# Hybrid encoder trunk: pre-norm token factors applied behind the input and up projections instead of ahead of them

## The chip, the cores and the metric

The kernel runs on one core of one Trainium2 chip. The core has a matrix engine (PE, with its weight loads shown as PEld), a vector engine (DVE), a scalar engine (ACT), a general engine (POOL) and an engine that here only issues transfers (SP). Each works through its own instructions in order and waits on semaphores for the others. Products land in PSUM banks; everything else lies in SBUF. The metric is the device time of one execution in microseconds, as the median of the runs; the profile is of one execution.

## The reference

Two layers on a residual stream x of 512 tokens by 1024 channels, in float32. Cut to what matters:

```python
def rms_norm(x, g):
    y = x * rsqrt(mean(x * x, axis=-1) + 1e-6)
    return y * g

for l in range(2):
    h = rms_norm(x, g_pre_mix[l])
    q_a, k_a, v_a, q_b, k_b, v_b, q_m, gate_pre = split(h @ w_in[l])
    o_a = neighborhood_attention(q_a, k_a, v_a, rpb[l])        # 6 heads
    o_b = dilated_attention(q_b, k_b, v_b)                     # 3 groups of 2 heads, mixed
    o_m = memory_attention(q_m, rms_norm(mem, mem_norm_g), w_mem_kv[l])
    gates = sigmoid(gate_pre + b_gate[l])                      # 3 x 1024
    merged = gates[0] * (o_a @ w_br_a[l]) + gates[1] * (o_b @ w_br_b[l]) + gates[2] * (o_m @ w_br_m[l])
    x = x + rms_norm(merged @ w_out[l], g_post_mix[l])
    h = rms_norm(x, g_pre_ffn[l])
    a, b = split(depthwise_conv(h @ w_up[l], conv_w[l], conv_b[l]))
    x = x + rms_norm((gelu(a) * b) @ w_down[l], g_post_ffn[l])
```

An RMS norm multiplies by a weight per channel and by a factor per token. The factor per token is the same for all channels, so it can stand on either side of a product over the channels.

## The kernel before

Activations lie with channels on partitions: x is eight tiles of 128 channels by 512 tokens, and a projection tile is 128 output channels by 512 tokens in one PSUM bank. To keep float32 accuracy every operand is split into a high part (a rounded copy, made by ACT) and a low part (the rest, made by DVE or POOL, `split`, L220), and a product is three matmuls: high by high, high by low, low by high (`mm3`, L246). A tile over all 512 tokens is 24 matmuls of 512 columns for a depth of 1024 (`linear`, L257); a tile done by halves (`HALVES`, 256 tokens each) is 48 matmuls of 256 columns (`run_group`). Weights come in by SP transfers of 512 KB into three `wraw` buffers and are split (`weights`, L224).

A planner, `Woven` (L46), writes the order of PE's instructions. It keeps a clock `clk` of estimated PE cost. Side work is written as generators ("jobs"): a job issues some instructions, then yields a delay in microseconds of that clock or a flag's name, and is taken up again when its due time has passed at the next `tick`, which comes after each depth step of a product. `give` sets a flag, and `need` takes up jobs until a flag is set. PE's order is exactly the order in which the program issues its instructions, so an instruction of PE that waits holds up all that was issued behind it. The order on DVE, ACT and POOL is fixed when the program is built: of the instructions ready at a time, one that the program issued earlier goes first. `Counted` (L99) estimates the time up to which ACT and DVE have work, and `ready` (L183) turns that into a delay.

A token factor is made by `rstd_job` (L323): two small products with a column of 1/1024 sum the squares over the partitions into a `pt` bank, ACT takes the root, DVE the reciprocal and two diagonal matrices of it, and a product of a matrix of ones with these spreads the factor to all partitions. `pre_norm_job` (L347) then makes h = x times weight times factor, and its split, for one half of the tokens; a flag `h...` lets the projection of that half start. `end_job` (L361) ends a sub-layer for one half: the factor of the post-norm, then for each x tile a multiply, an add to x, a square and the sum of squares, and after a delay the pre-norm of what follows.

Stages of a layer: a group of six leading input tiles by halves (`FIRST`, `group_banks` with six banks); the memory keys and values (for layer 0 behind the group, for layer 1 ahead of it, with the memory's norm done during layer 0's w_down); the remaining projections interwoven with the attention heads (`attention_job`); 24 gate tiles with the branch products (`gated`, L717); w_out with all eight tiles by halves; a group of six leading up tiles by halves, whose weights POOL splits; the other 38 up tiles with convolution and GELU (`conv`, L730); w_down with the last tile (layer 0) or the last two (layer 1) by halves (`sublayer_end`, L741). The projections' results are taken out of PSUM by `a_q`, `a_k`, `a_v`, `b_q`, `b_k`, `b_v`, `m_q`, `gated` and `conv`, which read the bank directly.

## Time and profile before

| | us |
|---|---|
| median of the runs | 1579.56 |
| lowest and highest of three runs | 1579.55, 1582.83 |
| the profiled execution | 1579.04 |
| its span, first to last instruction | 1577.3 |

| engine | busy us | share of the span | instructions |
|---|---|---|---|
| PEld | 1316.4 | 83% | 8246 |
| DVE | 911.2 | 58% | 1654 |
| ACT | 727.4 | 46% | 1289 |
| POOL | 186.4 | 12% | 244 |

How to read it: busy time is the time in which an engine had an instruction running. Matmuls are pipelined, so a row of one matmul is longer than the distance to the next, and the rate is read from long runs of them in the chain of waits. A row of the timeline gives start, duration, engine, line, operation, output and inputs by the program's names, shapes and a count when equal neighbours are merged; in brackets stands the idle time ahead of it and who ended it. Nearly all ACT and DVE instructions show L114, the line of the helper that counts them, so tiles rather than lines tell them apart: `mm`, `s`, `o` and `pt` are PSUM banks, `h` and `m` are SBUF tiles for split activations and weights, `y` scratch tiles, `acc` and `sq` sums of squares and squares, `st` small columns. `wraw`, `whi` and `wlo` are a raw weight tile and its parts.

### The profile page before, as it was taken

The page shows a single profiled execution, that of the slowest core. Times are in us where ns is not written, and L with a number is a line of the kernel's source. Part 1 is how long each engine was busy: PE and PEld are TensorE (multiplying, and loading weights), DVE is VectorE, ACT ScalarE, POOL GpSimd, SP SyncE. Part 2 cuts the span into 40 slices and gives each one's busy share as a digit, 9 for nine tenths or more (in the row PEclk, how much of TensorE's full clock was granted, in tenths as well). Part 3 has the DMA queues.
Part 4 walks back from the last instruction along what each step waited for, and adds up shares of the span by engine and source line. Part 5 has one row for each costly group of instructions (what it writes and reads, how often), then busy time and mean ns, then how long its engine had stood idle before and what let it go on. Part 6 is the DMA issues. An engine that isn't in the chain of part 4 may idle for free.

```text
span 1577.3 us, 21375 instructions
## 1 busy us (share of the span) xinstructions
PE 1529.7 (97%) x8246; PEld 1316.4 (83%) x8246; DVE 911.2 (58%) x1654; ACT 727.4 (46%) x1289; POOL 186.4 (12%) x244
## 2 busy tenths in 40 slices
PE   6999999999999999999989999999999999999997
PEld 5988888889898888878888888888898888888887
DVE  6686566344866666542386856743457666664233
ACT  5465575334544444532345646733454544444231
POOL 4340000110400000010062300001121000000000
PEclk9999999999999999999999999999999999999998
DMA  7222213224213222333331221132431232223331
GB/s 241 87 78 67 66 56 100 88 94 134 81 42 106 93 95 96 115 97 100 115 113 49 86 69 56 51 120 74 140 101 48 69 105 95 94 96 96 99 103 62
DMA packets 46614, 144.96 MB, mean 92 GB/s; under 512 B 5232, under 2 KB 11376, under 8 KB 46512
## 3 DMA queue, kind: packets, MB, share of 16 engines
q1 hardware_dynamic: 44656, 139.61, 27.7%
q10 hardware_dynamic: 1152, 2.10, 0.5%
q0 software_dynamic: 704, 1.88, 0.4%
q8 instruction: 65, 1.06, 0.3%
q14 instruction: 37, 0.30, 0.1%
HBM read 141.47 MB, written 2.10 MB: 91 GB/s over the span
## 4 chain that ended last, share of the span: by engine, by line
PE 88%; DVE 8%; ACT 2%; issue 1%; DMA 1%; SPq 0%; ACTq 0%
PE mm L244 73%; PE s L244 6%; PE o L244 3%; PE pt L244 2%; DVE h L114 2%; PE pt L255 2%; DVE y L114 2%; DVE x L114 1%; DVE m L114 1%; DVE wlo L114 1%; ACT whi L114 1%; DVE acc L114 1%; DVE ka L114 0%; ACT y L114 0%; DMA m<-in_memT_dram 0%
## 5 line engine op out<-in xcount | busy, mean ns | idle before, releaser
L244 PE MATMUL mm<-h,whi 128*128 128x512 f32 x2432 | 755.7, 392 | 0.0
L244 PEld LDWEIGHTS mm<-h,whi 128*128 128x128 f32 x2432 | 449.6, 188 | 88.7
L114 DVE TENSOR_TENSOR wlo<-wraw,whi 128x1024 fp32r<-128x1024 f32 (+1 forms) x203 | 246.9, 1218 | 394.9 <-ACT whi L114 394.8
L244 PE MATMUL mm<-h,wlo 128*128 128x512 f32 x1216 | 473.9, 390 | 0.0
L114 ACT CAST whi<-wraw 128x1024 fp32r<-128x1024 f32 (+1 forms) x203 | 210.3, 1038 | 296.5 <-PE mm L244 295.7
L244 PEld LDWEIGHTS mm<-h,wlo 128*128 128x128 f32 x1216 | 228.2, 188 | 48.5
L244 PE MATMUL mm<-m,whi 128*128 128x512 f32 (+1 forms) x672 | 178.2, 354 | 1.6 <-DVE m L114 0.8
L244 PEld LDWEIGHTS mm<-m,whi 128*128 128x128 f32 x672 | 119.6, 192 | 19.0 <-PE mm L244 1.3
L114 DVE SCALAR_TENSOR_TENSOR y<-mm,vec,y 128x511 f32<-128x511 f32 x160 | 118.9, 746 | 8.5 <-ACT y L114 5.9
L244 PE MATMUL mm<-m,wlo 128*128 128x512 f32 (+1 forms) x336 | 118.3, 352 | 0.7 <-DVE wlo L114 0.7
L114 ACT ACTIVATE y<-mm,vec 128x512 f32<-128x512 f32 (+1 forms) x163 | 113.6, 698 | 0.1
L244 PE MATMUL mm<-m,m 128*128 128x512 f32 (+1 forms) x432 | 88.6, 346 | 0.0
L222 POOL TENSOR_TENSOR m<-wraw,m 128x512 fp32r<-128x512 f32 x42 | 56.3, 1355 | 238.5 <-ACT m L114 234.2
L728 POOL TENSOR_TENSOR m<-m,y 128x512 f32<-128x512 f32 x28 | 36.1, 1289 | 405.7 <-DVE y L114 405.7
L244 PEld LDWEIGHTS mm<-m,m 128*128 128x128 f32 x432 | 67.6, 190 | 8.4
L244 PEld LDWEIGHTS mm<-m,wlo 128*128 128x128 f32 x336 | 64.4, 192 | 9.4 <-DVE wlo L114 1.1
L114 ACT ACTIVATE y<-y 128x512 f32<-128x512 f32 x44 | 27.8, 632 | 87.3 <-DVE y L114 87.3
L244 PE MATMUL mm<-h,m 128*128 128x256 f32 x456 | 63.6, 296 | 4.0 <-ACT h L114 1.6
L114 DVE TENSOR_TENSOR acc<-acc,sq 128x256 f32<-128x256 f32 (+1 forms) x86 | 44.6, 521 | 37.5 <-ACT sq L114 36.9
L114 ACT CAST m<-wraw 128x512 fp32r<-128x512 f32 (+1 forms) x98 | 56.1, 602 | 21.1 <-DMA wraw<-in_w_brb_dram 9.5
L244 PEld LDWEIGHTS mm<-h,m 128*128 128x128 f32 x456 | 59.2, 199 | 6.4 <-ACT h L114 2.8
L114 ACT CAST m<-pt 128x512 fp32r<-128x512 f32 (+1 forms) x72 | 38.2, 539 | 40.4 <-PE pt L255 32.0
(150 smaller groups left out, 1835.8 us busy)
## 6 DMA issues: line engine op xcount, KB each, us to landing
wraw<-in_w_in_dram SPq DMA_DIRECT2D x88, 512.0 KB, 3.3
wraw<-in_w_up_dram SPq DMA_DIRECT2D x88, 512.0 KB, 3.3
wraw<-in_w_down_dram SPq DMA_DIRECT2D x32, 512.0 KB, 3.5
wraw<-in_w_out_dram SPq DMA_DIRECT2D x16, 512.0 KB, 3.4
wraw<-in_w_down_dram SPq DMA_DIRECT2D x16, 384.0 KB, 3.1
wraw<-in_w_kv_dram SPq DMA_DIRECT2D x8, 512.0 KB, 3.6
wraw<-in_w_bra_dram SPq DMA_DIRECT2D x16, 192.0 KB, 2.3
x<-in_xT_dram SPq DMA_DIRECT2D x8, 256.0 KB, 7.2
```

The lines of the kernel that those rows point to most:

```text
L114: return op(*args, **kw)
L222: last_lo[eng or V] = (eng or V).tensor_sub(lo, src, f32(hi)).ins
L244: wv.pe(nc.tensor.matmul(ps, a, b, start=first, stop=last), cost)
L255: wv.pe(nc.tensor.transpose(ps[:, 128 * i:128 * i + 128], s, ident), 0.11)
L728: (V if br == 2 and m >= 6 else G).tensor_add(acc[m], acc[m], gs)
```

## The change

The token factor of both pre-norms leaves the projection's input. x times the norm's weight is split directly (`raw_split`), products run on that, and the factor is kept as a tile R (128 by 512, the same in all partitions) by which each projection result is multiplied on its way out of PSUM (`scaled`, on DVE). R is made by `factor_job` behind the sums of squares; results that are ready before R are held with their banks (`evacuate`, `release`). `end_job` now issues multiply, add and the two split parts for each of eight x tiles, gives the flag, then the squares, and then the factor job. The factor is spread by a product of the broadcast reciprocal column with the identity, without DVE's diagonal matrices. Leading groups have four tiles instead of six; w_out has two tiles by halves instead of eight; leading weights are loaded and split (by DVE) between the whole tiles of w_out and w_down. The memory norm and its products stand behind the first six input tiles in both layers, ahead of the seventh. At the start, `vec` comes by ACT's queue, and x and the first weights are loaded in interleaved pieces. The pool `hp` is gone and `mp` has 48 buffers. The planner's cost of a matmul of n columns is (max(n, 256) + 32) / 2400.

```diff
-FIRST = (0, 3, 6, 1, 4, 7)
+LEAD_IN, LEAD_UP = (0, 3, 6, 1), (0, 22, 1, 23)
...
+    vec = const.tile([128, depth, V_N], F32, name="vec")
+    nc.scalar.dma_start(out=vec, in_=vecs)
...
-        cost = max(n, 256) / 2400.0
+        cost = (max(n, 256) + 32) / 2400.0
...
         V.reciprocal(rs, rs)
-        diag = small("h32", 4, (128, n))
+        yield 0.8
         for b in range(nb):
-            V.tensor_scalar_mul(diag[:, 128 * b:128 * b + 128], ident, rs[:, b:b + 1])
-        yield 1.2
-        mm(pr, ones, diag, True, True, n * 4 / 2400.0)
+            one = rs[:, b:b + 1]
+            wide = bass.AP(one.tensor, one.offset, [list(one.ap[0]), [0, 128]])
+            mm(pr[:, 128 * b:128 * b + 128], wide, ident, True, True, 0.22)
         box.append(pr)
...
-    def pre_norm_job(l, goff, acc, hs, i):
+    def raw_split(l, goff, k, cols, h):
+        g = vec[:, l, goff + k:goff + k + 1]
+        ACT.activation(h[0][:, cols], x[k][:, cols], AF.Copy, scale=g)
+        V.scalar_tensor_tensor(out=h[1][:, cols], in0=x[k][:, cols], scalar=g, in1=f32(h[0][:, cols]),
+                               op0=ALU.mult, op1=ALU.subtract)
+
+    def factor_job(l, goff, accs, i, R):
         half, box = HALVES[i], []
...
+        yield from rstd_job(accs, 256, box)
+        ACT.copy(R[:, half], box[0])
+        if i == 1:
+            yield 0.6
+            wv.give(f"R{l}.{goff}")
...
+    def scaled(ps, R, scale=None):
+        y = ytile()
+        if scale is None:
+            V.tensor_mul(y, ps, R)
+        else:
+            V.scalar_tensor_tensor(out=y, in0=ps, scalar=scale, in1=R, op0=ALU.mult, op1=ALU.mult)
+        return y
...
+    def end_job(l, goff, og, acc, i, nxt, lat, more=()):
         half, box = HALVES[i], []
         yield lat
         yield from rstd_job([acc[:, half]] + list(more), 256, box)
         for k in range(KD):
             V.tensor_mul(og[k][:, half], og[k][:, half], box[0])
...
+                raw_split(nxt[0], nxt[1], k, half, nxt[2][k])
+            if k == 0:
+                first = max(ACT.t, V.t)
+        if nxt is None:
+            return
+        yield max(0.5, first - wv.clk + MARGIN)
+        wv.give(f"h{nxt[0]}.{nxt[1]}.{i}")
+        acc2 = nxt[4]
+        for k in range(KD):
+            sumsq_add(acc2[:, half], x[k][:, half], k == 0)
+        yield ready(1.0)
+        yield from factor_job(nxt[0], nxt[1], [acc2[:, half]], i, nxt[3])
...
     def group_banks():
-        return [mmbank(), mmbank(), sbank(), sbank(), obank(128), tbank()]
+        return [sbank(), sbank(), obank(128), mmbank()]
...
-        gs = ytile()
+        gs = scaled(psg, R)
...
+        u, y = scaled(ps, R), ytile()
...
-            wv.spawn(end_job(l, goff, og, acc, acc2, i, None if then is None else (lambda i: then(acc2, i)), lat[i], more))
+            wv.spawn(end_job(l, goff, og, acc, i, nxt, (1.4, 1.8)[i], more))
...
+    for i in range(2):
+        wv.spawn(factor_job(0, V_PRE, first_squares(HALVES[i]), i, R), (13.0, 20.0)[i])
...
+        hm, km, vm = [], [], []
+        wv.spawn(mem_norm_job(l, hm, big), 22.0)
...
+                if n == 6:
+                    mem_kv(l, hm, km, vm)
+                ps = pss[n] if n < len(pss) else proj(l, 3 * i + pr, hs, fence if n < 6 else None)
+                n += 1
+                evacuate(flag, lambda evac=evac, ps=ps, more=[f"va{l}.{pr}"] if i == 2 else []: evac(ps, R, qkva, *more))
+                if n > len(pss):
+                    release(5)
...
+        sublayer_end(l, V_POST, lambda m, i: [lambda: weights(w_out[l, m], KD, 128, None if i is None else ktile)],
+                     ms, 2, (l, V_PREF, hs, R, acctile()),
+                     [lambda m=m: gw.extend(group_weights([w_up[l, m]], (V,))) for m in LEAD_UP])
...
-            sublayer_end(l, V_POSTF, w_of, fs, 1, then, (1.4, LAT1), lambda: wv.spawn(kv_ahead()))
...
+            lead = [lambda m=m: gw.extend(group_weights([w_in[l + 1, m]], (V,))) for m in LEAD_IN]
+            hs = h_tiles()
+            sublayer_end(l, V_POSTF, w_of, fs, 1, (l + 1, V_PRE, hs, R, acctile()), lead[:3])
+            lead[3]()
```

More of the change, by code (lines that the diff above doesn't have):

```diff
@@ L359, in post_norm_tile @@
         ACT.activation(og[m][:, cols], ps, AF.Copy, scale=vec[:, l, goff + m:goff + m + 1])
-    def end_job(l, goff, og, acc, acc2, i, then, lat, more=()):
+    def end_job(l, goff, og, acc, i, nxt, lat, more=()):
         half, box = HALVES[i], []
@@ L747, in sublayer_end @@
         acc = acctile()
-        acc2 = acctile() if then is not None else None
         n0 = KD - n_half
         total = len(rhs)
-        def one(m, ps, parts, cols, first):
-            k0 = 0
-            for w in parts:
+        fill = list(fill)
+        for m in range(n0):
+            ps, k0 = mmbank(), 0
+            for w in w_of(m, None):
                 w = w()
-                linear(ps, w, rhs, cols, 0, k0, total)
+                linear(ps, w, rhs, FULL, 0, k0, total)
                 k0 += len(w)
-            post_norm_tile(l, goff, m, ps, og, acc, cols, first)
-        for m in range(n0):
-            one(m, mmbank(), w_of(m, None), FULL, m == 0)
+            post_norm_tile(l, goff, m, ps, og, acc, FULL, m == 0)
+            if m > 0 and fill:
+                fill.pop(0)()
         ws = {m: [p() for p in w_of(m, m - n0)] for m in range(n0, KD)}
-        if mid is not None:
-            mid()
         more = []
@@ L834, in tile_hybrid_encoder @@
             acc[m] = big(F32)
[L835 removed]
+            gated(l, 0, m, hs, R, weights(w_bra[l, m], 3, 128, big), 0, oa, acc)
         for m in range(KD):
@@ L876, in tile_hybrid_encoder @@
             fs.append((hi, lo))
+        for j in range(NFF):
+            pair = []
+            for m in (j, j + NFF):
+                if m in pss:
+                    pair.append(pss[m])
+                else:
+                    n += 1
+                    w = weights(w_up[l, m], KD, 128, after=fence if n <= 2 else None)
+                    pair.append(mmbank())
+                    linear(pair[-1], w, hs)
+            evacuate(flag, lambda j=j, pair=pair: mixed(j, *pair))
+            if j >= 2:
+                release(0)
         def w_of(m, i):
             return [lambda p0=p0, pn=pn: weights(w_down[l, m, :, p0:p0 + pn, :], pn, 128,
-                                                 htile if i is not None and (i == 1 or p0 == 16) else None)
+                                                 big if i is not None and (i == 1 or p0 == 16) else None)
                     for p0, pn in ((0, 8), (8, 8), (16, 6))]
```

251 lines of the change are left out of this document (106 added, 145 removed).

## The prediction

> **What bounds the kernel now.** I read the page first, then busy time by stage (bounds from the timeline), then who waits for whom on PE, then the timeline where PE waits.
>
> ```profile
> span 1577.3 us, 21375 instructions
> ## 1 busy us (share of the span) xinstructions
> PE 1529.7 (97%) x8246; PEld 1316.4 (83%) x8246; DVE 911.2 (58%) x1654; ACT 727.4 (46%) x1289; POOL 186.4 (12%) x244
> ```
>
> PE is busy 1529.7 of 1577.3 us, so removing waits can win 47.6 us at most. The stages show where they lie (columns: stage; its length, then busy us and instructions of PE, PEld, DVE, ACT and POOL; PE clock; DMA share; GB/s), and PE's waits on whom:
>
> ```profile
> 0.00:15.00 15.00, 3.03 (x10) 2.28 (x10) 5.18 (x14) 7.03 (x16) 7.32 (x36) 1.00 0.81 267
> 15.00:71.50 56.50, 52.58 (x402) 51.38 (x403) 42.18 (x86) 28.49 (x66) 22.82 (x31) 1.00 0.42 140
> 260.00:374.00 114.00, 114.00 (x525) 95.17 (x524) 46.71 (x59) 41.64 (x59) 18.04 (x14) 1.00 0.34 109
> 369.05:458.55 89.50, 84.97 (x697) 83.83 (x696) 61.68 (x130) 45.92 (x104) 16.16 (x12) 1.00 0.24 77
> 464.00:656.00 192.00, 192.00 (x848) 158.97 (x847) 116.44 (x141) 84.04 (x107) 0.00 (x0) 1.00 0.29 96
> 782.16:847.17 65.01, 59.07 (x480) 57.94 (x479) 52.83 (x114) 32.16 (x76) 33.30 (x56) 1.00 0.29 94
> 847.17:1040.00 192.83, 189.78 (x1007) 158.14 (x1006) 130.94 (x323) 119.66 (x241) 23.47 (x32) 1.00 0.21 68
> 1144.70:1236.36 91.66, 87.79 (x698) 86.44 (x697) 61.64 (x130) 46.01 (x104) 16.12 (x12) 0.96 0.24 76
> ```
>
> ```profile
> PE pt L244 <- DVE y L114: 11.6, 3, 9.9
> PE pt L244 <- DVE h L114: 9.7, 8, 3.0
> ...
> PE mm L244 <- DVE wlo L114: 0.7, 1, 0.7
> ```
>
> Up-projection (464 to 656) and gates (260 to 374) leave PE no gap: there, matmul time alone counts. PE lacks work for 15.9 us up to 71.5, where the first memory products end; for 4.5 and 3.9 us in the two stages from w_out's first tile to the six leading up tiles; for 5.9 us from half 0 of layer 0's last w_down tile to the end of layer 1's first six tiles; and for 3.1 us in an attention stage. The tile waited with is nearly always pt, the bank of a token factor. Those waits are what the change can touch; the rest is matmul rate.
>
> **Terms that are plain.**
>
> ```profile
> 1156.29 2.88 PE mm L244 x24
> ```
>
> ```profile
> 257.60 111.97 PE mm L244 x495
> ```
>
> ```profile
> L114 DVE TENSOR_TENSOR y<-mm,y 128x512 f32<-128x512 f32 x32 | 21.9, 684 | 0.0
> ```
>
> In the chain, 24 matmuls of 256 columns take 2.88 us (0.12 each), 495 of mostly 512 columns 111.97 (0.226 each). A tile in two halves costs 5.76 us, a whole one 5.43. Six w_out tiles a layer and two tiles in each of four leading groups become whole: 20 x 0.33 = 6.6 us less for PE, counted inside the stage sums below.
>
> The added multiply is priced by y<-mm,y (128x512 from PSUM, 684 ns): one more on DVE per projection tile. The up stage holds 35 tiles, so DVE goes from 116.4 to 140 of 192 us, hidden beside PE; the gates' 21 tiles take it from 46.7 to 61 of 114, hidden too. Uncovered, each tile would cost its 0.684. An attention stage has 20 such tiles, 13.7 us: DVE 131 becomes 145 of 193, and there PE does wait for softmax pieces in DVE's queue; but the heads now start before the memory products, with more matmul work to lie between. Bounds per layer: -3 (all its waits gone) and +7 (half of 13.7 shows). I take +0.5, because 62 us of DVE are free there now: **+1** for both.
>
> PE's wait for wlo (0.7) at the start of w_down comes while layer 1's memory norm crowds ACT; that norm moves away: **-0.7**. At the very end two diagonal products leave DVE: **-0.5**. The leading up weights' loads move ahead on SP, between w_out tiles; that stage has DMA share 0.24, so they hide.
>
> **The start.** The timeline has PE's first projection product, and the first after the memory products:
>
> ```profile
> 15.10 0.58 PE L244 MATMUL mm<-h,m 128*128 128x256 f32 x1 [1.01 <-ACT h L114]
> ```
>
> ```profile
> 71.53 0.63 PE L244 MATMUL mm<-h,whi 128*128 128x512 f32 x2
> ```
>
> Afterwards the first one needs vec (moved from POOL's queue to ACT's), two x tiles and half a weight tile, 0.7 MB; at the 267 GB/s of the first 15 us (4.0 MB) and some 2 us to a first landing, about 6 us with the split. The first pair of tiles follows the arrival of 2.3 MB, to about 12; the second needs 4.2 MB, about 16, and takes 5.8; half 1 takes 11.5 and two factor jobs 1.6: 35. Two whole tiles (10.9) and memory products (11.5 + 0.8) give 58. But the memory norm's factor now stands in PE's queue right ahead of those products, which all queue behind it, and its root, reciprocal and eight pairs of DVE operations come after the evacuation of six tiles and the first head's softmax in DVE's. Bounds 0 and 9; I take 5.5 (2.5 to the factor, then eight steps that DVE does in 0.73 and PE in 0.36). With 0.7 of stray waits 64.5 against 71.5: **-7**.
>
> **Between sub-layers.** Prices from the timeline:
>
> ```profile
> 1552.32 0.17 DVE L114 RECIPROCAL st<-st 128x2 f32<-128x2 f32 x1 [1.94 <-ACT st L114]
> 1552.52 0.48 DVE L114 TENSOR_SCALAR h<-ident,st 128x128 f32<-128x128 f32 x2
> 1553.99 0.42 DVE L114 TENSOR_TENSOR y<-y,pt 128x256 f32<-128x256 f32 x1 [0.99 <-PE pt L244]
> ```
>
> ```profile
> 1205.00 0.76 DVE L114 TENSOR_TENSOR x<-x,y 128x256 f32<-128x256 f32 x2
> ```
>
> ```profile
> 1217.43 1.26 DVE L114 SCALAR_TENSOR_TENSOR h<-x,vec,pt 128x256 f32<-128x256 f32 x3 [0.99 <-PE pt L244]
> ```
>
> ```profile
> 1179.66 1.51 DVE L114 TENSOR_TENSOR x<-x,y 128x256 f32<-128x256 f32 x1
> ```
>
> Reciprocal to first multiply is 1.67 us, about 1.1 without the diagonal pair. Two adds of 128x256 take 0.76, so 0.335 each in a row; three scalar_tensor_tensor 1.26, so 0.395 each. The add of 1.51 ran while POOL split weights; leading weights move to DVE, so I take 0.335 throughout. Per x tile, end_job now does multiply, add and low part, 1.065 us: 8.5 for a half, with seven adds of squares, 2.35, behind it. ACT's parts hide under these.
>
> DVE takes first what the program issued first, once it is ready:
>
> ```profile
> 415.43 0.39 ACT L114 ACTIVATE sq<-mm 128x256 f32<-128x256 f32 x1 [0.53 <-PE mm L244]
> ```
>
> ```profile
> 418.69 0.42 DVE L114 TENSOR_TENSOR h<-h,h 128x256 fp32r<-128x256 f32 x1
> 419.02 0.42 DVE L114 TENSOR_TENSOR acc<-acc,sq 128x256 f32<-128x256 f32 x1
> ```
>
> ```profile
> 807.90 0.26 ACT L114 ACTIVATE st<-pt,eps 128x2 f32<-128x2 f32 x1 [0.59 <-PE pt L244]
> ```
>
> ```profile
> 809.62 0.42 DVE L114 TENSOR_TENSOR h<-h,h 128x256 fp32r<-128x256 f32 x1
> 809.95 0.16 DVE L114 RECIPROCAL st<-st 128x2 f32<-128x2 f32 x1
> ```
>
> A w_out square is ready at 415.8, but its add runs at 419.02, behind the norm's earlier-issued products; end_job's root is ready at 808.2 and its reciprocal runs at 809.95. In the new order this decides. Let T be the end of half 0 of the last w_out tile.
>
> Half 0's chain starts on DVE at T+3.05. PE does half 1 of only two tiles (eight before, 23 us) and is done at T+6.5. The next half's sums are placed 1.8 us on by the planner, so after three k steps of the group, at T+8.7. They need the add of the last tile, issued after chain and squares: 3.05 + 8.5 + 2.35 + two adds = T+14.6. PE waits 5.9, all group matmuls queued behind. That half's chain then runs from T+17 to T+25.5. The factor job of half 0 is placed at planner time 13.9, its broadcast at 15.3, which PE reaches at about T+21.3; its reciprocal was issued after the second chain and comes at T+25.7. PE waits 4.4 more; 16.5 us of group follow: T+42.4. Six whole tiles and two halves before T are 38.4, two more up tiles 10.9: 91.7, against 89.5 and 91.7 now. So **+2.2** in layer 0 and **0** in layer 1. R itself is needed only after the group and hides.
>
> At the layer boundary T is 782.16. Half 1 of one tile (66 products) ends at T+8.7; the sums wait from 10.8 to 14.3; the second chain runs from 16.6 to 25.1; half 0's broadcast waits from 18.9 to 25.4. Then 18.8 of broadcast and group, 10.9 for two tiles, 12.3 of memory products and the same 5.5 for the memory norm (done during w_down before, at no cost): 72.9 against 65.0, **+7.9**.
>
> Then the clock (fourth column, after PE's busy time):
>
> ```profile
> 1182.00:1186.00 4.00, 1.68 (x14) 1.00 0.35 127
> 1186.00:1188.00 2.00, 1.72 (x10) 0.57 0.00 0
> 1188.00:1192.00 4.00, 3.39 (x14) 0.50 0.42 135
> 1192.00:1194.00 2.00, 2.00 (x14) 0.73 0.00 0
> ```
>
> After a stretch with little work PE's granted clock is 0.5 for about 6.6 us, which costs 3.3; layer 0's like stage did not pay it. With waits of 4 us and more I add half of it, 1.5, in each of four places (start, both w_out stages, boundary): **+6**.
>
> Sum: -7 + 2.2 + 0 + 7.9 - 0.7 - 0.5 + 1 + 6 = +8.9. The profiled execution took 1579.04 (1.7 around its span), so 1587.9; the median of the runs is 0.5 above it: **1588**. Own range of this case 1578 to 1599: memory wait 0 to 9 at both layers, clock 0 to 13.
>
> **Rivals.**
>
> Faster: the reciprocals get through. If DVE has gaps while its chain waits for ACT's high parts, half 0's reciprocal slips in and only the first wait stays: w_out stages 38.4 + 37.5 + 10.9 = 86.8 (-2.7 and -4.9), boundary 63 (-2), memory wait 3 (start -9.5), clock +3: about 1564; without the first wait too, near 1550. It decides whether a reciprocal follows its root within 0.5 us. For it: DVE is busy 53 of 65 us in the boundary stage, so gaps exist. Against it: the two late rows above. Chance 0.34.
>
> Clock: every wait over 3 us halves it. Six such waits (two at start and boundary, the last one in each w_out stage) at 3.3 are 20 instead of 6: 1602. One of two like stages dropped so far, at waits of 2.3 and 0.9; chance 0.08. The Trainium skill, TensorE: Matmul & The Clock Gate, section "What's actually happening", says that a free-running window of about 3.4 us of PE activity sets the clock to half or full; by that rule each of the six would drop it. The trace agrees in the 0.50; it does not show a wait this long after the start.
>
> Attention: half of DVE's 13.7 us shows in both layers, +14 instead of +1: 1601. Against it: 3.1 us of waits now. Chance 0.08.
>
> That the change does what it says I don't doubt: the pre-norm factor gates no group matmul, only the post-norm's does.
>
> **Numbers.** 0.50 for the forecast, 0.34, 0.08, 0.08. The range 1563 to 1602 leaves out the wait-free end and the worst of clock and attention. A measurement tells about 0.2%, 3.2 us, from no change: faster takes the first rival and a little of the forecast, 0.36; same 0.12; slower 0.52.
>
> **What would show it.** Right: in each w_out stage two PE waits of 4 to 6 us with pt, for DVE's acc and reciprocal; a PE wait ahead of both memory products; the first product before 7 us; the up stage without PE gaps and DVE near 73%. Wrong: pt waits under 2 us, or gaps of PE in the up stage or the gates.

## The result, and the profile after

The changed kernel takes 1620.07 us (median; 1618.84 to 1620.62), the kernel before beside it 1579.55: a ratio of 1.0251, 95% interval 1.0233 to 1.0268. It is 40.5 us slower. The forecast was slower, at 1588 with a range up to 1602: the side was right, the size was not.

The page of the kernel after, its span and busy times:

```profile
span 1618.6 us, 20293 instructions
PE 1543.1 (95%) x7802; PEld 1307.6 (81%) x7802; DVE 999.5 (62%) x1749; ACT 744.0 (46%) x1241; POOL 128.4 (8%) x193
```

PE's idle time grew from 47.6 to 75.5 us, 27.9 more. But PE is also 13.4 us longer *busy*, with 444 matmuls fewer. That is the first thing to see: fewer matmuls took longer, because more of them ran at a lower clock. By stage (stage; its length, then busy us and instructions of PE, PEld, DVE, ACT and POOL; PE clock; DMA share; GB/s):

```profile
0.00:40.40 40.40, 30.35 (x216) 28.66 (x217) 21.71 (x48) 22.98 (x56) 4.88 (x33) 1.00 0.63 208
40.40:81.40 41.00, 32.23 (x188) 28.36 (x187) 34.31 (x82) 26.03 (x53) 20.25 (x30) 0.83 0.27 89
81.40:270.85 189.45, 181.50 (x942) 149.46 (x941) 135.87 (x301) 109.84 (x207) 18.23 (x23) 0.99 0.22 67
382.10:475.25 93.15, 85.27 (x516) 77.04 (x515) 58.70 (x117) 47.47 (x91) 0.00 (x0) 0.96 0.25 79
480.00:672.00 192.00, 192.00 (x848) 158.97 (x847) 140.11 (x177) 86.85 (x107) 0.00 (x0) 1.00 0.31 98
795.70:884.00 88.30, 72.32 (x478) 68.08 (x477) 65.15 (x162) 47.18 (x108) 26.33 (x54) 0.86 0.19 60
884.00:1072.68 188.68, 181.15 (x940) 149.34 (x939) 133.79 (x300) 109.72 (x207) 19.45 (x23) 0.99 0.22 68
1184.00:1277.50 93.50, 85.63 (x518) 77.31 (x517) 58.95 (x117) 47.83 (x91) 0.00 (x0) 0.96 0.25 78
```

The trace records a granted clock of 0.50 in pieces. Half of PE's busy time inside these pieces is what the lower clock cost: 4.0 us in the second row, 9.6 at the layer boundary, 2.7 and 2.6 in the two w_out stages, 22.3 over the whole span, against 3.4 before. (The column of the clock is a mean over the row, also over time in which PE stood; busy time times what it lacks of 1.00 is a rougher count.)

The rows show 1.00 for the start too, but there it is no measurement: the trace's first record of the clock lies at 15.39 us, and up to it PE ran at half rate. 17 products of 256 columns in a row took 3.79 us there, 18 later ones 2.32:

```profile
11.77 3.79 PE L240 MATMUL s<-m,m 128*128 128x256 f32 x17
...
25.01 2.32 PE L240 MATMUL s<-m,m 128*128 128x256 f32 x18
```

The kernel before has the same up to 22.32 us, its first record. By half of PE's busy time up to there, an estimate, it is 3.4 us here and 4.6 before. With it the lower clock costs some 17.8 us more than before, and the 41.3 us of span are 27.9 of idle time and 17.8 of lower clock, less 4.4 of matmul work that the change saves (by difference).

Where they lie, from the start of the gates and the end of the six up tiles in both traces: start to layer 0's gates +13.2 us (270.85 against 257.60), gates to the six up tiles +3.5, from there to layer 1's gates +23.1, the next two stretches +1.3 and +0.2. PE's waits:

```profile
PE pt L240 <- DVE acc L110: 15.4, 3, 5.4
PE pt L240 <- DVE st L110: 13.2, 4, 7.5
PE pt L240 <- ACT m L110: 10.3, 3, 5.6
...
PE pt L251 <- DVE y L110: 7.8, 10, 1.5
PE o L240 <- DVE m L110: 5.9, 6, 2.0
```

The first and third rows are the two waits that the forecast saw in each w_out stage and at the boundary, for half 1's sum of squares and for half 0's factor. The view puts the third down to ACT, but what PE's broadcast needs is DVE's reciprocal, which at the boundary ends 0.15 us before it, 6.5 us after its root, behind half 1's chain:

```profile
818.18 0.26 ACT L110 ACTIVATE st<-pt,eps 128x2 f32<-128x2 f32 x1 [3.57 <-PE pt L240]
...
824.93 0.16 DVE L110 RECIPROCAL st<-st 128x2 f32<-128x2 f32 x1
...
825.24 1.19 PE L240 MATMUL pt<-ident,st 128*128 128x128 f32 x4 [5.55 <-ACT m L110]
```

The second row is mainly the wait ahead of the memory products (7.5 us in layer 0, 4.2 in layer 1). The last two are the attention heads' transposes and value products.

The wait of 7.5 us is seen on three engines: PE's sums of the memory's squares and the broadcast behind them, ACT's queue in between, and DVE's reciprocal.

```profile
52.30 0.50 PE L240 MATMUL pt<-mean,h 128*128 128x1 f32 x4
...
60.86 1.22 PE L240 MATMUL pt<-ident,st 128*128 128x128 f32 x4 [7.49 <-DVE st L110]
```

```profile
56.65 1.28 ACT L110 ACT_TABLE_LOAD   x1 [1.83 <-DVE st L110]
57.94 0.51 ACT L110 ACTIVATE y<-y,st 128x256 f32<-128x256 f32 x1
...
59.05 1.28 ACT L110 ACT_TABLE_LOAD   x1
60.35 0.26 ACT L110 ACTIVATE st<-pt,eps 128x2 f32<-128x2 f32 x1
```

```profile
60.64 0.17 DVE L110 RECIPROCAL st<-st 128x2 f32<-128x2 f32 x1 [0.37 <-ACT st L110]
```

The sums are done at 52.8, the root runs at 60.35: ACT's order has the first head's exponentials ahead of it, which wait for DVE, and a table load of 1.28 us on either side. The planner had put the broadcast 0.8 us behind the sums, so PE stood.

### The profile page after: what moved, and what is told of

The parts are those of the page before. It is cut to its first block, busy times and chain, and to the rows that moved or that the text cites. A ratio compares the mean times of both kernels' runs of the same rounds, so it can differ in the third digit from the quotient of the medians.

```text
span 1618.6 us, 20293 instructions
## 1 busy us (share of the span) xinstructions
PE 1543.1 (95%) x7802; PEld 1307.6 (81%) x7802; DVE 999.5 (62%) x1749; ACT 744.0 (46%) x1241; POOL 128.4 (8%) x193
## 4 chain that ended last, share of the span: by engine, by line
PE 83%; DVE 10%; ACT 4%; issue 2%; DMA 1%; SPq 0%; ACTq 0%; DVEq 0%
PE mm L240 74%; PE s L240 3%; DVE m L110 3%; DVE y L110 3%; PE o L240 3%; PE pt L251 1%; ACT m L110 1%; PE pt L240 1%; DVE wlo L110 1%; ACT y L110 1%; DVE x L110 1%; DVE ka L110 1%; ACT L110 1%; DVE st L110 1%; ACT whi L110 0%
## 5 line engine op out<-in xcount | busy, mean ns | idle before, releaser
L240 PE MATMUL mm<-m,whi 128*128 128x512 f32 (+1 forms) x3424 | 1036.2, 385 | 2.4 <-DVE m L110 1.3
L240 PEld LDWEIGHTS mm<-m,whi 128*128 128x128 f32 x3424 | 632.2, 189 | 123.5 <-DVE m L110 3.1
L240 PE MATMUL mm<-m,wlo 128*128 128x512 f32 (+1 forms) x1712 | 655.6, 383 | 0.0
L240 PEld LDWEIGHTS mm<-m,wlo 128*128 128x128 f32 x1712 | 323.9, 189 | 63.2
L110 DVE TENSOR_TENSOR y<-mm,R 128x512 f32<-128x512 f32 x136 | 93.6, 688 | 142.7 <-PE mm L240 142.7
L110 DVE SCALAR_TENSOR_TENSOR y<-y,vec,y 128x511 f32<-128x511 f32 x176 | 130.5, 748 | 3.3 <-ACT y L110 0.6
L240 PE MATMUL mm<-m,m 128*128 128x256 f32 (+1 forms) x528 | 110.4, 337 | 0.6 <-DVE m L110 0.6
L110 ACT ACTIVATE y<-y,vec 128x512 f32<-128x512 f32 x136 | 105.7, 780 | 9.0 <-DVE y L110 8.6
L240 PE MATMUL s<-m,m 128*128 128x256 f32 (+2 forms) x480 | 77.6, 316 | 10.1 <-ACT m L110 8.0
L240 PE MATMUL o<-m,m 128*128 128x256 f32 (+2 forms) x448 | 78.2, 299 | 5.9 <-DVE m L110 5.9
L110 DVE TENSOR_TENSOR m<-pt,m 128x512 fp32r<-128x512 f32 (+1 forms) x72 | 45.2, 630 | 22.3 <-ACT m L110 20.3
```

The source lines that it names most:

```text
L110: return op(*args, **kw)
L240: wv.pe(nc.tensor.matmul(ps, a, b, start=first, stop=last), cost)
```

## The experiments

Each is the kernel after with the edit shown, unless it says otherwise; "after" is 1620.07 us, ratio 1.0251. Beside the runs the kernel before took 1578.4 to 1580.0 us, and the ratios are to that. In a cut edit, `...` stands for lines left out. The first ones ask where the waits come from.

**e1: the memory norm earlier.**

```
-        wv.spawn(mem_norm_job(l, hm, big), 22.0)
+        wv.spawn(mem_norm_job(l, hm, big), 12.0)
```

> The memory norm is planned 10 us earlier in both layers (delay 12 instead of 22); nothing else. Theory 'root behind exponentials': its root runs late on ACT because the first head's exponentials and two table loads of 1.28 us are ordered ahead of it, and PE stands at its broadcast. Earlier in the plan it is ordered ahead of them: PE's waits ahead of the memory products (8.5 us in layer 0, 5.4 in layer 1 with the small ones behind) fall under 1.5 each, and the half clock that follows them (5.3 and 3.6 us of PE time) goes too: 1620 becomes about 1598. Rival 'DVE has no room': the wait only moves to the eight memory products' high and low parts, or ahead of the leading group: 1612 or more. Rival 'the clock drops anyway': only the waits go, 1607.

Measured 1617.81 us, ratio 1.0237 (1.0222 to 1.0253): not told apart from after. PE's waits of e1:

```profile
PE mm L240 <- DVE wlo L110: 8.7, 2, 4.9
```

The wait for the root is down to 1.8 us, and PE waits instead for the low parts of the memory's weights, behind evacuations and the first head on DVE. Theory missed, first rival right.

**e2: extra products in the wait.** `rstd_job` issues them ahead of the broadcast, into the broadcast's half of the bank.

```
...
+        for i in range(fill[1] if fill else 0):
+            mm(pr, fill[0][:, 0:128], fill[0][:, 0:256], True, True, 0.0)
         for b in range(nb):
             one = rs[:, b:b + 1]
...
```

> PE is given 62 (layer 0) and 36 (layer 1) extra products of 256 columns right ahead of the memory norm's broadcast, into the bank that the broadcast overwrites: 7.4 and 4.3 us at 0.12 each, about the length of its two waits there. The waits stay, PE only doesn't stand still. Theory 'a long stand halves the clock': granted clock stays 1.00 where it was 0.50 (60 to 70 and 863 to 872 us), and 5.3 + 3.6 us come back, less 1 to 2 for products that outlast the wait: about 1613. Rival 'the clock drop is not from the stand' or 'the drop is made up for later': 1620 to 1622.

Measured 1629.56 us (ratio 1.0312, 1.0297 to 1.0328). The experiment missed its aim: the products waited for the same root, since ACT reads the sums from their bank, and ran behind the wait:

```profile
59.60 9.83 PE L240 MATMUL pt<-m 128*128 128x256 f32 x62 [7.26 <-ACT st L110]
```

It decides nothing about the clock; e7 and e15 do it over.

**e3: w_out's last four tiles by halves.** The loads of the four leading up weights begin one tile earlier for it, and of the four halved tiles only two keep their weights in the buffers that both of them had (`ktile`).

```
...
-                     ms, 2, (l, V_PREF, hs, R, acctile()),
+                     ms, 4, (l, V_PREF, hs, R, acctile()),
...
-            if m > 0 and fill:
+            if fill and (m > 0 or n_half == 4):
```

> w_out's last four tiles are done by halves instead of two (both layers), so PE has 11.5 us of half 1 while half 0's chain runs on DVE, not 5.8. Theory: the wait of 5.4 us for half 1's sum of squares in each w_out stage falls to 0 to 2, the half clock after it (2.7 and 2.3 us lost) goes, two more tiles in halves cost 0.66 a layer; the wait of 2.4 for the factor's reciprocal stays: 1607 to 1610. Rival 'DVE's two chains are the bound': what PE gains it waits for at half 1's first low part or at the reciprocal: 1616 to 1621.

Measured 1605.49 us (ratio 1.0161, 1.0145 to 1.0176), 14.6 less and a little better than expected. The wait for `acc` in each w_out stage fell from 5.4 us to two of 1.3 and 1.2. The later one, which was expected to stay, went too: half 0's broadcast now comes together with half 1's. So too few products between half 0's chain and half 1's sums are the cause of the first wait.

**e4: no token factor in the attention stages.** The seven evacuations read the bank as before, for example:

```
...
-        stack_split(scaled(ps, R, -0.125), tiles)
+        stack_split(ps, tiles, -0.125)
```

> The queries, keys and values of the attention stages are taken straight from the banks, as before the change, on ACT and DVE: the token factor is left out of them (the gates and the up-projection keep it). Theory 'DVE's added multiplies show': the attention stages' PE waits go from 8.0 and 7.8 us back to about 3.2 each, the drop of the clock after the 2.0 us wait near their end goes, and with six evacuations shorter the memory norm's wait shrinks by 2 or 3: 1600 to 1606. Rival, the forecast's own 'the multiplies hide beside PE' (the attention stages lose to the heads' new order instead): 1617 to 1621.

Measured 1624.67 us (ratio 1.0280, 1.0263 to 1.0297). Most of layer 0's attention stage:

```profile
80.00:272.50 192.50, 180.96 (x929) 147.71 (x928) 122.09 (x282) 107.89 (x211) 13.13 (x21) 0.99 0.20 65
```

DVE has 14 us less to do than in the stage after (135.87) and PE still stands 11.5 us. Taking the added multiplies away alone does not shorten the waits of this stage (e12 takes them away together with the booking). Ahead of layer 0's memory products the wait did shrink, from 7.5 to 1.8 us, but transposes wait 2.3 behind it, and at the boundary 5.6 became 6.7.

**e5: the old booking.** The change also booked every matmul 32 columns longer in the planner; the forecast had passed over this line.

```
-        cost = (max(n, 256) + 32) / 2400.0
+        cost = max(n, 256) / 2400.0
```

> One line of the diff undone: the planner books a matmul with max(n, 256)/2400 us again, without the 32 columns that the change adds (6 per cent for a 512-column product). Nothing else. The planner then sees time pass more slowly and places each later piece of a job (softmax, transposes, factors) after more products. Theory 'shorter cover in the attention stages': the new booking is why transposes and value products wait there (8.0 and 7.8 us, 3.2 and 3.1 before the change), so undoing it gives 5 to 9 us over both stages and the drop of the clock near their end: about 1612. Rival 'order, not booking' (the heads now start ahead of the memory products): 1618 to 1622, waits where they are.

Measured 1628.02 us (ratio 1.0301, 1.0281 to 1.0320). The new booking helps, by about 8 us; the attention stage idles 10.7 us without it:

```profile
81.00:271.00 190.00, 179.33 (x932) 148.36 (x931) 134.76 (x299) 108.05 (x205) 14.93 (x22) 0.98 0.20 64
```

**e6: the memory products later**, behind the ninth tile, their broadcast 9 us behind the sums.

```
-        yield 0.8
+        yield lag
...
-        yield from rstd_job([acc], N_MEM, box)
+        yield from rstd_job([acc], N_MEM, box, 9.0)
...
-                if n == 6:
-                    mem_kv(l, hm, km, vm)
...
         release()
+        mem_kv(l, hm, km, vm)
```

> The memory norm's broadcast is placed 9 instead of 0.8 us behind its sums, and the memory products are moved behind the ninth projection tile (they stood behind the sixth), in both layers. Theory 'nothing but its place': PE has three more tiles (16 us) of work while ACT and DVE get to the root, the reciprocal, the memory's parts and the low parts of its weights, so the waits ahead of the memory products (8.5 and 5.4 us) fall under 2 each and the half clock behind them (5.3 and 3.6) goes: 1599 to 1604. Rival 'DVE's queue is the bound in the first 30 us of the stage': the waits come back at the added tiles' banks, at transposes or at low parts: 1614 to 1620.

Measured 1626.18 us (ratio 1.0292, 1.0277 to 1.0308): slower, and the rival's picture, by more than it said, in PE's waits:

```profile
PE pt L251 <- DVE y L110: 18.6, 14, 4.1
...
PE mm L240 <- DVE wlo L110: 11.5, 3, 6.0
```

**e7: extra products in a bank of their own.** As e2, but into the bank of the first memory tile, which `mem_kv` takes before it needs the memory's norm.

```
+        for i in range(fill[2] if fill else 0):
+            mm(fill[1][0], fill[0][:, 0:128], fill[0][:, 0:256], True, True, 0.0)
...
+        spare.append(mmbank((128, N_MEM)))
         wv.need(f"mem{l}")
...
-            ps = mmbank((128, N_MEM))
+            ps = mmbank((128, N_MEM)) if m else spare[0]
```

> As e2, but the extra products (64 and 38 of 256 columns, 7.7 and 4.6 us at 0.12) go to the bank that the first memory tile is about to use, which nothing else reads or writes, so that they run during the wait and not behind it. Theory 'a long stand halves the clock': the granted clock stays 1.00 behind both waits, 5.3 + 3.6 us come back, less about 1 for products that outlast the wait: 1612 to 1615. Rival 'the clock is not about the stand': 1620 to 1622.

Measured 1620.02 us (ratio 1.0253, 1.0236 to 1.0271): the rival's time, but not its reason. The products did run in the wait and ended with it, the clock stayed at 1.00 behind it as the theory had it, and fell later (a row of the timeline, then windows with the columns of the stages):

```profile
52.12 7.84 PE L240 MATMUL mm<-m 128*128 128x256 f32 x64
```

```profile
60.00:64.00 4.00, 1.86 (x12) 1.37 (x12) 3.32 (x10) 2.91 (x8) 2.14 (x3) 1.00 0.08 25
64.00:68.00 4.00, 3.59 (x17) 2.97 (x16) 3.92 (x12) 2.18 (x6) 0.00 (x0) 0.65 0.00 0
```

At full clock PE reaches the memory products sooner than DVE and ACT make their operands, stands 2.1 us there between 60 and 64, and drops to 0.50 from 65.2 us on. The total is as after, so there the half clock seems to have hidden beside DVE's pace; no run shows it.

**e8: half 0's factor job later.**

```
-        yield ready(1.0)
+        yield ready(1.0 if i else 14.0)
```

> Half 0's factor job is planned 14 us after its squares instead of 1, in both w_out stages and at the layer boundary; half 1's stays. Theory (the forecast's second wait): PE stands at that factor's broadcast with the group queued behind it because the reciprocal comes after half 1's chain on DVE; later in the plan, PE does the group meanwhile, and the waits of 2.4, 5.5 and 2.4 us go, with the half clock that the middle one causes (2.9): 1605 to 1609. Rival 'the chain of half 1 is the bound': the group's second half then waits for half 1's low parts instead: 1616 to 1620.

Measured 1609.86 us (ratio 1.0192, 1.0177 to 1.0207), just above the 1605 to 1609 expected: the waits of 2.4 us are gone, the one of 5.6 at the boundary is down to 2.0. The wait for the factor was a matter of where the broadcast stands in PE's queue.

The next four put things together.

**e9: the memory products first**, as before the change.

```
-        wv.spawn(mem_norm_job(l, hm, big), 22.0)
+        wv.spawn(mem_norm_job(l, hm, big), 6.0)
...
         fence = crit[0]
+        mem_kv(l, hm, km, vm)
...
-                if n == 6:
-                    mem_kv(l, hm, km, vm)
```

> The memory products are put back right behind the leading group, ahead of the two whole tiles, of all evacuations and of the heads, and their norm is planned 16 us earlier (delay 6), in both layers: the order of before, with the group still at four tiles. Theory 'order': the memory norm's root, parts and low weight parts run on ACT and DVE beside the group, ahead of the first head's softmax, so the waits ahead of the memory products (8.5 and 5.4 us) shrink to some 3 and 1 with no half clock behind them, and the attention stages' PE waits go from 7.9 and 7.5 us back toward 3.2, since the heads no longer run into the memory work: 1585 to 1595. Rival 'DVE's queue is the bound': the same DVE work only comes in another order, PE waits for low parts there or at the first heads: 1608 or more.

Measured 1616.50 us (ratio 1.0232, 1.0211 to 1.0254). It is 3.6 us under after, with intervals that overlap. Windows of e9, from about the end of the group past the memory products, and from there to the gates:

```profile
40.40:72.00 31.60, 29.93 (x185) 26.40 (x184) 27.75 (x60) 20.45 (x40) 20.02 (x25) 1.00 0.29 96
72.00:265.40 193.40, 182.27 (x943) 149.51 (x943) 139.55 (x318) 111.89 (x216) 20.71 (x27) 0.98 0.20 64
```

The memory products now cost 1.7 us of waits and no clock, but PE stands 11.1 us in the rest of the stage, where it had stood 7.9. Layer 0's gates start 5.4 us earlier (25 to 35 had been expected of both layers together), and layer 1 gains nothing: its boundary's waits are longer, 6.5 and 6.0 us where they were 4.6 and 5.6, in PE's waits from 790 to 860 us:

```profile
PE pt L240 <- DVE acc L110: 6.5, 1, 6.5
PE pt L240 <- ACT m L110: 6.0, 1, 6.0
```

The theory missed.

**e10: e3 and e8. e11: e9 and e10.**

> e3 and e8 together: w_out's last four tiles by halves, and half 0's factor job 14 us later. Theory: the two waits of the w_out stages are separate, the gains add: 1620 - 14.5 - 10 = 1595. Rival 'one chain behind both': with one wait gone the other had already shrunk: 1601 to 1605.

> e9 and e10 together. If each wait has its own cause and its own half clock, the gains add to 1560 to 1570, below the kernel before (1580). Rival 'DVE is the bound behind the group': about 1585 to 1595, no faster than before.

Measured 1613.19 us (ratio 1.0213, 1.0198 to 1.0228) and 1608.67 (1.0189, 1.0174 to 1.0204). Both lie above everything that was expected of them: the gains do not add, and e10 is slower than e3. Its timeline shows why: 14 us later, half 0's reciprocal falls behind half 1's chain again, and PE stands for it.

```profile
444.38 0.87 DVE L110 SCALAR_TENSOR_TENSOR m<-x,vec,m 128x256 fp32r<-128x256 f32 x2
...
445.51 0.15 DVE L110 RECIPROCAL st<-st 128x2 f32<-128x2 f32 x1
```

```profile
445.81 1.19 PE L240 MATMUL pt<-ident,st 128*128 128x128 f32 x4 [5.49 <-DVE st L110]
```

A placement is right only for the order around it.

**e12: the attention stages as before in all but the group:** e9, e4 and e5 together.

> e9 with the attention's evacuations as before the change (the token factor left out of queries, keys and values, as in e4) and the planner's old booking (as in e5): everything of the attention stage as before but the four-tile group. Theory 'order alone': the attention stages' PE idle time is 3 to 4 us here and in e9 alike, times within 5 us of e9's. Rival 'added multiplies or booking': e9's attention stages still idle 7 us or more and this one's 3 to 4, 8 to 12 us faster than e9.

Measured 1612.70 us (ratio 1.0212, 1.0196 to 1.0227), 3.8 us under e9, with intervals that overlap. The two attention stages:

```profile
72.00:263.30 191.30, 184.84 (x967) 152.54 (x966) 132.33 (x316) 114.56 (x232) 20.67 (x28) 0.99 0.21 65
880.00:1069.70 189.70, 183.24 (x956) 151.49 (x957) 130.98 (x306) 113.06 (x223) 16.31 (x24) 0.99 0.22 67
```

PE stands 6.5 us in either, between the 3.1 of before and the 11.1 of e9. Neither side's numbers are met: in e9's order multiplies and booking together make 4.6 us of a stage's 11.1, which of the two is not shown, and they are a part of the attention's loss at most. What is left may lie with the four-tile group or with how the heads fall between the tiles; no run tests either.

The last ones are for what stayed open: the clock, DVE's queue, and the attention.

**e13: the memory weights' low parts on POOL**, on top of e1. **e14: e3 and e9. e16: e14 with e13's edit.**

```
-            w = weights(w_kv[l, m], KD, 128)
+            w = weights(w_kv[l, m], KD, 128, eng=G)
```

> e1 with the low parts of the memory weights taken on POOL instead of DVE (four of 128x1024 a layer, 1.2 to 2.4 us each on DVE). Theory 'DVE's queue is the bound behind the group': in e1 PE's waits moved to just these low parts (4.9 and 3.8 us); off DVE they and the half clock behind them (2.3 us each) go, and 5 to 6 us of DVE time a layer with them: 1618 becomes 1603 to 1609. Rival 'POOL is no faster': POOL takes about 2.7 us for one (1.36 for half of it before the change), has bias tables to prepare, and slows DVE while it runs: 1614 to 1622.

> e3 and e9 together (without the later factor job of e8, which cost e10 its gain). Theory: the w_out wait and the memory's place lie in different stages, so the gains add: 1605.5 - 4 to 6 = 1600 to 1602. Rival, as in e10 and e11: one gain takes the other's place: 1605 or more.

> e14 with the memory weights' low parts on POOL, as in e13. Theory 'DVE's queue': beside the group POOL is idle and DVE is not, so the memory products no longer wait and the evacuations behind them start earlier: 4 to 8 us under e14. Rival: as e14 within 2, or slower by the time that POOL needs more for each.

Measured: e13 1616.00 us (ratio 1.0234, 1.0214 to 1.0253), e1 within its interval; e14 1600.83 (1.0139, 1.0118 to 1.0159), as if the gains of e3 and e9 added, though its interval overlaps e3's; e16 1603.45 (1.0158, 1.0142 to 1.0175), no better than e14. In e13 PE waits for POOL instead, which needs 2.4 us for each part:

```profile
PE mm L240 <- POOL wlo L211: 9.1, 3, 4.9
```

```profile
L211 POOL TENSOR_TENSOR wlo<-wraw,whi 128x1024 fp32r<-128x1024 f32 x8 | 19.4, 2424 | 1.7 <-ACT whi L110 1.3
```

So moving this work from DVE to POOL did not cure the start of the attention stages. Whether less work would is not shown, since a part takes POOL about twice as long.

**e15: PE kept busy ahead of half 1's sums**, on top of e8.

```
...
+        for i in range(40 if fill else 0):
+            mm(pr, fill[:, 0:128], fill[:, 0:256], True, True, 0.0)
         for i, a in enumerate(accs):
...
```

> e8 with 40 extra products of 256 columns (4.8 us at 0.12) ahead of half 1's sums in both w_out stages and at the boundary, in the bank that the sums and the broadcast use next; their results are overwritten. They run during the waits of 5.4, 4.6 and 5.4 us. Behind these, PE has a group of products ready whose length alone sets the stage. Theory 'the half clock costs its own time': the clock stays 1.00 there and 2.8 + 2.4 + 2.7 us come back: 1602 to 1604. Rival 'the chain of half 1 hides it' (PE, sooner through the group's first half, waits for the second): 1608 to 1612.

Measured 1600.89 us (ratio 1.0142, 1.0127 to 1.0158; e8's is 1.0192, 1.0177 to 1.0207), 9 us less with 120 products *more*, somewhat better than the theory's 1602. The same stretch of layer 0's w_out stage in e8 and in e15:

```profile
432.00:436.00 4.00, 0.00 (x0) 0.00 (x0) 3.93 (x11) 2.51 (x7) 0.00 (x0) 1.00 0.00 0
436.00:440.00 4.00, 2.80 (x13) 2.83 (x14) 1.87 (x6) 1.16 (x4) 0.00 (x0) 0.50 0.00 0
440.00:444.00 4.00, 4.00 (x25) 4.00 (x25) 2.16 (x7) 1.04 (x3) 0.00 (x0) 0.64 0.02 6
```

```profile
432.00:436.00 4.00, 3.52 (x30) 3.32 (x29) 3.36 (x9) 2.36 (x7) 0.00 (x0) 1.00 0.00 0
436.00:440.00 4.00, 4.00 (x36) 4.00 (x35) 2.72 (x8) 1.52 (x4) 0.00 (x0) 1.00 0.01 2
440.00:444.00 4.00, 4.00 (x35) 4.00 (x35) 4.00 (x13) 2.85 (x7) 0.00 (x0) 1.00 0.00 0
```

In four busy microseconds PE does 25 matmuls behind the stand, where the clock is 0.64, and 35 or 36 without it. This is the half clock's own price, shown: half 1's sums wait for DVE's chain in both, and only the standing is gone.

**e17: a wider margin in the plan.**

```
-MARGIN = 0.3
+MARGIN = 1.0
```

> The margin that the planner adds to its estimate of ACT's and DVE's end, before it lets PE take up a result (transposes, value products, factors), is 1.0 instead of 0.3 us; nothing else. Theory 'the plan's estimate is too short for the fuller DVE': attention stages' PE idle falls from 7.9 and 7.5 us to 5 or less each, and the drop of the clock near each stage's end goes: 1608 to 1614. Rival 'the waits follow DVE's total, not the plan': 1617 to 1624, idle as before.

Measured 1618.74 us (ratio 1.0248, 1.0231 to 1.0265), as after. The two attention stages stand 8.8 and 9.4 us, so a wider margin alone does not help; layer 0's:

```profile
81.00:270.00 189.00, 180.18 (x940) 148.76 (x939) 133.10 (x299) 107.43 (x206) 17.78 (x24) 0.99 0.21 67
```

**e18: what helped, together.** e14, with e8's delay and e15's products at the layer boundary alone.

> e14, and at the layer boundary alone e8's later factor job and e15's 40 extra products ahead of half 1's sums. Theory: the boundary's second wait (5 us) and the half clock behind both of its waits (2.5 and 2.3 us in e14) go: 1600.8 becomes 1591 to 1594, the shortest of the versions of the change and still over the kernel before (1580), because the start of layer 0 and the attention stages stay as they are. Rival 'the gain is taken by the memory products behind it', which DVE paces: 1597 to 1601.

Measured 1594.57 us (ratio 1.0094, 1.0076 to 1.0112): the shortest version of the change, 25.5 us under it, and still 15 over the kernel before. PE idles 55.4 us in it and loses 11.9 in the pieces at 0.50; before it was 47.6 and 3.4.

## Why the prediction was right or wrong

Step by step, as the forecast put them.

- **First product before 7 us: right** (6.32). **The group done by 35 us: wrong**, it took until 40.4. The first pair of tiles ended at 18.2 us where 12 was worked out, the second at 25.0 (21.8), and half 1 took 15.4 (13.1). One reason is the price of a product, 0.12 us from the first one on: up to 15.39 us it was 0.22, which by an estimate is 1.6 us for the 17 products above and at most 3.4 for all. The rest stays open. This term was mis-sized by 5.4.
- **The memory norm's factor in PE's queue: right mechanism.** Taken at 5.5 us with bounds 0 and 9, it was 8.5 in layer 0 (7.5 and two small ones) and 5.4 in layer 1. The forecast's reason (root and reciprocal late behind evacuations and the first head's softmax) is the one seen, though the queue that holds the root is ACT's, where the forecast named DVE's; the table loads on ACT it had not counted.
- **w_out stages: right, the total in part by luck.** Forecast +3.7 and +1.5 with the clock, measured +3.5 and +1.3; the first wait 5.4 where 5.9 was worked out, the second 2.4 where it was 4.4. e3 and e8 show both causes. Shorter waits and a larger price of the clock (2.7 and 2.6 instead of 1.5) partly cancel. The first rival, with a chance of 0.34, had the reciprocals slip in within 0.5 us of their roots; 6.5 us lie between them at the boundary.
- **Layer boundary: waits right, total wrong.** 3.5 + 6.5 + 5.5 = 15.5 us of waits were forecast; 4.6 + 5.6 + 5.4 came. The stage took 88.3 us where 72.9 and 1.5 of clock were worked out. Of the 13.9 missing, 8.1 are the clock behind these waits (9.6); by an estimate 3.4 are the first head's products that now stand in this stretch (16 score products at 0.12, 16 transposes at 0.09); the rest stays open.
- **Clock, +6: the term that failed most.** "I add half of it, 1.5, in each of four places" became some 17.8 us. All six stands of 4.2 us or more between the first product and the last were followed by a granted clock of 0.50. The rival "every wait over 3 us halves it" had the right mechanism and nearly the right price, 20, and was given a chance of 0.08; its 1602 fell short only because the terms above and below were short too. The forecast took an even chance from two like stages of the kernel before, of which one had dropped. Both had a stand of the same 2.3 us; they differ in where it lay on a fixed grid of 3.41 us, and on that grid a stand of 4 us always tells (last section). The Trainium skill (TensorE: Matmul & The Clock Gate, "What's actually happening") has the clock halved after an idle window of about 3.4 us that runs freely. An estimate from that figure: only a stand of 6.8 us would hold a whole window for sure and one of 2 us none, so the forecast's reading, that each of its six waits would drop the clock, does not follow from that section. The trace agrees with the window that runs freely, but is harsher: all six from 4.2 us on dropped, and some of 2.0 too, so less than a whole idle window was enough here.
- **Attention, +1 for both layers: wrong.** PE's idle time went from 3.05 to 7.5 us in layer 1 and likewise in layer 0, +9.2 in all, and a stand of 2.0 us near each stage's end cost another 1.7 of clock in each. The rival "half of DVE's 13.7 us shows" had the size (+14), but its cause is not shown: without the multiplies alone (e4) the waits are no shorter. Nor does the old booking (e5) or a wider margin (e17) alone shorten them, and the memory's place (e9) brings part of its gain back as new waits. Only in e9's order did leaving out multiplies and booking together take 4.6 us off a stage (e12). What makes the heads wait 4 to 5 us more a layer stays open.
- **Up stage and gates: right.** No gaps of PE; DVE 140.11 of 192 us where 140 was worked out. The multiplies hide there.
- **Up stage and w_down together: mis-sized on the good side,** -3.2 instead of -0.7, from the six up tiles' end to half 0 of the last tile (320.45 us against 323.61).

In sum: the stretches to the gates were forecast at -5 and +9.2 and came at +13.2 and +23.1, 32 us in all. Clock makes about 14 of it, attention waits 8, the group 5.4, layer 0's memory wait 3; up stage and w_down gave 2.5 back, and some 4 stay open. The forecast's own range, 1578 to 1599, was narrower than the bounds it names: a memory wait of 0 to 9 us at both layers and a clock of 0 to 13 reach from 1571 to 1602.

## What to carry to other kernels

A wait of PE costs its length and then, if it lasts some 4 us, the half clock behind it: in this kernel every such stand cost its length plus 2.6 to 4 us. Price it so, not at an average over luck, unless what follows is paced by another engine anyway (e7). When a factor moves out of the way of a product, look at what lay *between*: here 23 us of products by halves had covered the post-norm's chain on DVE, and cutting them to 6 uncovered it. A gain shown alone (e3, e8) is not a gain together (e10); try the sum.

## What the runs showed of the hardware that was not expected

- Where a stand lies decides, beside its length. In each of the 20 traces the pieces at 0.50 begin, and all but the last end, at multiples of 3.41 us from one another. Cut at these marks, two stands show it, of 2.0 us at 245 and of 2.4 us at 447 in the kernel after (PE's busy time and instructions, its clock, DMA share and GB/s). The first lies inside one stretch; the second reaches into the next, and the clock stays:

```profile
244.08:247.49 3.41, 1.39 (x7) 1.00 0.00 0
247.49:250.90 3.41, 3.41 (x13) 0.50 0.44 141
445.47:448.88 3.41, 1.67 (x14) 1.00 0.00 0
448.88:452.30 3.42, 2.78 (x23) 1.00 0.00 0
```

In e7 the first stand is cut by a mark too, 2.79 and 2.02 us of work on its two sides, and 1.00 stays throughout. The two like stages of the kernel before differ in the same way: their stands of 2.3 us left 2.36 and 2.11 us of work in two stretches in layer 0, and 1.24 in one in layer 1, where the clock fell. Over all traces, behind the first record and at full clock: of 129 stretches with PE busy under 0.45, 128 were followed by 0.50; from 0.45 to 0.61, 11 of 68; above that none of 8822. An estimate from this: a lone stand of 3.8 us or more leaves at least 1.9 us idle in one stretch, and so is sure to drop the clock.

- The first products after the start ran at half rate, 0.22 us against 0.13 in the rows at 11.77 and 25.01, although the view shows a clock of 1.00 there: the clock's records begin only when the half rate ends. A distance between matmuls shows it where the column does not.
- Useless matmuls made a kernel faster: by an estimate 14.4 us of them (120 at 0.12), hidden in waits, 9 us gained (e15).
- A low part on DVE took longer while POOL worked: 1.69 us here, as POOL's three subtractions ran beside it. Of the 210 of that shape, the 194 with no POOL instruction beside them took 1.21 to 1.23; of the other 16, five took 1.37 to 1.79.

```profile
48.91 1.69 DVE L110 TENSOR_TENSOR wlo<-wraw,whi 128x1024 fp32r<-128x1024 f32 x1
```

```profile
48.79 3.55 POOL L546 TENSOR_TENSOR y<-mask,y 128x256 f32<-128x256 f32 x3 [1.98 <-DMA y<-in_rpb_dram]
```

The Trainium skill (SBUF — State Buffer, "SBUF: two separate sides") says that DVE with two SBUF inputs and GpSimd share a port pair that one holds for a whole instruction. These two rows agree with it in that both sides took longer (one of POOL's three took 1.71, where 27 of the 36 of its kind took under 0.8); no run here took POOL's work away to show it.
